# Two K chunks of a modulation product in one PE run, in a two-layer diffusion trunk on one NeuronCore

## The chip, the core and the metric

The kernel runs on one core of one Trainium2 chip. The metric is the device time of one execution in microseconds. Three runs of the kernel before took 1898.16, 1900.98 and 1904.77 us; the median is 1900.98.

## What is computed

The reference is a trunk of two layers over 256 latent tokens and 256 context tokens of width 1024. Each layer takes six modulation vectors from a conditioning vector, mixes the tokens in three branches (attention, a gated linear attention called GLA, a convolution), and ends in a feed-forward network. Cut to what matters here:

```python
mod = (silu_c @ w_ada[l] + b_ada[l])[:, None, :]
sh1, sc1, g1, sh2, sc2, g2 = jnp.split(mod, 6, axis=-1)
...
x = _post(x, _latent_mixer(_modulate(x, sh1, sc1), mem, cos, sin, p), g1, ln1_g[l], ln1_b[l])
x = _post(x, _ffn(_modulate(x, sh2, sc2), p), g2, ln2_g[l], ln2_b[l])
```

The product `silu_c @ w_ada[l]` has K = 1024 rows and 6144 columns. Its first 2048 columns (sh1, sc1) are made by one function, the other 4096 (g1, sh2, sc2, g2) by the one that is changed. The latent and the context conditioning vector are multiplied together, as the columns of one small stationary operand.

## The kernel before

PE does the large projections as three float32r products each: a weight chunk of 128 x 1024 values (512 KB) is loaded into a `raw` buffer by SP's queue (L107), ACT writes its rounded high part `whi` (L98), DVE the rest `wlo` (L99), and PE multiplies high by high, high by low and low by high (`mm`, L137). One feature-major group (`fm`, L153) is one such chunk and 24 matmuls. There are five `raw` buffers, three `whi` and two `wlo` (L54). A `raw` buffer of a weight chunk is free as soon as ACT and DVE have split it.

The modulation products are not split: they are plain float32 matmuls whose stationary operand is the conditioning vector (`self.sc[:, k, :]`, 128 x 32) and whose moving operand is the raw weight itself. Each output is 32 rows by 512 columns, and four of them (`gg` = 0 to 3) lie side by side on the 128 partitions of one PSUM bank. Their `raw` buffers come from the same five, and are free only when PE has multiplied them.

`ada_head` (L254) makes the first third of a layer's vectors, with its own operation line L280. In layer 0 it multiplies two K chunks for all four `gg` in one run of eight matmuls, from separate buffers and in the reverse order of loading. `ada_gen` (L294) makes the other two thirds, once with r = 1 and once with r = 2 for each layer, so it is called four times. It is a generator: at every `yield` it hands control back, and `step` (L872) takes one piece of it after each projection group, so that its transfers and products are spread between the groups. Behind the eighth piece it adds the bias (L311), transposes the sum through PE (L314), copies it into columns (L317) and stores two rows for later (L328).

The order of the work is the order of the program as a scheduler with priorities sorts it: weight loads and their splits are hoisted far ahead (`self.ahead = 3000`), evictions less far (`EVAC`), while the pieces of `ada_gen` stand about where they are written. Every engine and SP's queue then run in their fixed order.

The four calls lie in different surroundings. The first (layer 0, r = 1; 283 to 387 us in the trace) goes with the first half of the branch phase, where the convolution's taps (L679) and a GLA head share DVE. The second (layer 0, r = 2; from 484 us) goes with the convolution's branch, whose partial sums travel through DRAM (`mgold`, L1058, and `mgd`, L1066). The third and the fourth (layer 1, r = 1 and 2; 860 to 1000 us) are appended at L1162 behind `ada_head` of layer 1 and run in the feed-forward network of layer 0, with `raw<-in_wff` as the weight stream.

Of the kernel before, what the change touches and what calls it, by code (L numbers as in the profile page):

```python
# [21 lines left out]
KC = 8  # L22
# [30 lines left out]
class Trunk:  # L53
# [240 lines left out]
    def ada_gen(self, l, r, res):  # L294

        nc, I = self.nc, self.I
        ps = self.PS("mm")
        for k in range(KC):
            for hf in range(2):
                raw = self.T("raw", [128, 1152])  # L300
                c0 = (r - 1) * 2048 + hf * 1024
                nc.sync.dma_start(out=raw[:, :1024], in_=I["w_ada"][l, k * 128:(k + 1) * 128, c0:c0 + 1024])
                for g in range(2):
                    gg = 2 * hf + g
                    nc.tensor.matmul(ps[32 * gg:32 * gg + 32, :], self.sc[:, k, :], raw[:, g * 512:(g + 1) * 512],  # L305
                                     start=(k == 0), stop=(k == KC - 1))
            yield
        b = self.T("tB", [128, 512])
        nc.sync.dma_start(out=b, in_=I["b_ada"][l, r - 1])
        m = self.T("tB", [128, 512])  # L310
        nc.vector.tensor_tensor(out=m, in0=ps, in1=b, op=ALU.add)  # L311
        tr = self.PS("tr", (128, 4, 128))
        for t in range(4):
            nc.tensor.transpose(tr[:, t, :], m[:, t * 128:(t + 1) * 128], self.ident)  # L314
        mc = self.T("mc", [128, 32], name="modcol")
        for s in range(2):
            nc.vector.tensor_copy(  # L317
                mc[:, s * 16:(s + 1) * 16].rearrange("p (g t) -> p g t", g=4),
                tr.rearrange("p t (g s r) -> p s g t r", g=4, s=2)[:, s, :, :, 0])
        if r == 2:  # L320
            for s in range(2):
                nc.vector.tensor_scalar(out=mc[:, s * 16:s * 16 + 8], in0=mc[:, s * 16:s * 16 + 8],
                                        scalar1=1.0, scalar2=None, op0=ALU.add)

        for s in range(2):
            for n in range(2):
                row = 32 * (n + 2 * (r - 1)) + 16 * s
                nc.sync.dma_start(out=self.grow[2 * l + r - 1][s:s + 1, n * 512:(n + 1) * 512], in_=m[row:row + 1, :])  # L328
        res[(l, r)] = mc
        yield  # L330
# [961 lines left out]
```

## Time and profile before

| | |
|---|---|
| median of three runs | 1900.98 us |
| the profiled execution's own time | 1894.05 us |
| its span in the trace | 1892.3 us |
| granted TensorE clock, mean | 0.99 |
| TensorE (PE) busy | 1803.7 us, 95% |
| VectorE (DVE) busy | 1301.5 us, 69% |
| ScalarE (ACT) busy | 869.6 us, 46% |
| L305 on PE, 128 matmuls in 256 records | 35.1 us |
| bytes moved | 291.50 MB, 154 GB/s over the span |

The profile is one execution, traced. Busy time of PE counts pipelined matmuls with modelled ends, so a busy PE is not one at its peak. PEld is the load of stationary operands. A row of the groups by line names line, engine, operation, output and input tiles, shape and count, then busy time and mean duration in ns, then the idle time of the engine just before and what ended it. A row of the timeline starts with the start in us and the duration in us; a bracket at its end holds the idle time before it and its releaser. SPq is SP's DMA queue: its rows are issues, not transfers. An fp32 matmul leaves two records, so a run of four matmuls shows as x8.

### The profile page before, as it was taken

To read this page: it belongs to the slowest core of one execution; us is meant where nothing else is said; L and a number is where in the kernel's file an instruction comes from. 1 tells how busy PE (TensorE), PEld (TensorE's weight loads), DVE (VectorE), ACT (ScalarE), POOL (GpSimd) and SP (SyncE) were. 2 spreads that over 40 slices of the span, in tenths; PEclk is the share of its full clock that TensorE was granted. 3 is DMA by queue.
4 is the path that set the end of the run, shared out by engine and by line. 5 is a ranking of instruction groups with operands and counts; after the bars stand their busy time and mean duration, and the time that the engine had idled before them with its cause. 6 is when DMAs were issued, how large, how long until landed. Compare 5 with 4: busy or idle time off the path is not lost.

```text
span 1892.3 us, 29210 instructions
## 1 busy us (share of the span) xinstructions
PE 1803.7 (95%) x11260; PEld 1490.2 (79%) x11260; DVE 1301.5 (69%) x2266; ACT 869.6 (46%) x1498; POOL 189.9 (10%) x267
## 2 busy tenths in 40 slices
PE   6999999999999999989999999989999899979998
PEld 3777787777777878767768888877898789969996
DVE  4797999985743444864334457799999877676656
ACT  4455435434833333453222234556555476445442
POOL 0320000113002001000000001131000200210000
PEclk9999999999999999999999999999999999989999
DMA  8311124623374344576673367643233445755563
GB/s 322 99 56 56 57 69 142 206 85 91 122 253 134 101 135 145 196 259 219 204 240 107 103 214 237 210 126 91 91 112 116 143 128 164 238 196 172 195 205 120
DMA packets 90603, 291.50 MB, mean 154 GB/s; under 512 B 10320, under 2 KB 12112, under 8 KB 90464
## 3 DMA queue, kind: packets, MB, share of 16 engines
q1 hardware_dynamic: 90464, 289.64, 46.8%
q8 instruction: 88, 1.44, 0.3%
q14 instruction: 51, 0.42, 0.1%
HBM read 276.99 MB, written 12.62 MB: 153 GB/s over the span
## 4 chain that ended last, share of the span: by engine, by line
PE 74%; DVE 14%; ACT 5%; issue 3%; DMA 2%; POOL 2%; SPq 0%; POOLq 0%; DVEq 0%; ACTq 0%
PE mm L137 62%; DVE acc L679 5%; DVE wlo L99 4%; PE sd L453 2%; PE sd L427 2%; PE mm L305 1%; PE sd L614 1%; PE sd L641 1%; PE sd L561 1%; ACT whi L98 1%; PE sd L280 1%; PE tr L448 1%; DMA ada<-in_w_ada 1%; DMA raw<-in_wff 1%; DVE u L784 0%
## 5 line engine op out<-in xcount | busy, mean ns | idle before, releaser
L99 DVE TENSOR_TENSOR wlo<-raw,whi 128x1024 fp32r<-128x1024 f32 (+1 forms) x376 | 469.8, 1251 | 312.5 <-PE mm L137 221.8
L137 PE MATMUL mm<-hi,whi 128*128 128x512 f32 (+1 forms) x1904 | 649.8, 342 | 1.6 <-ACT whi L98 0.8
L137 PE MATMUL mm<-lo,whi 128*128 128x512 f32 (+1 forms) x1904 | 643.3, 338 | 3.1 <-DVE lo L358 2.9
L98 ACT ACTIVATE whi<-raw 128x1024 fp32r<-128x1024 f32 (+1 forms) x376 | 399.3, 1063 | 534.8 <-PE mm L137 384.2
L137 PE MATMUL mm<-hi,wlo 128*128 128x512 f32 (+1 forms) x1904 | 643.6, 338 | 0.5 <-DVE wlo L99 0.5
L137 PEld LDWEIGHTS mm<-hi,whi 128*128 128x128 f32 x1904 | 359.8, 189 | 59.7 <-issue 14.3
L137 PEld LDWEIGHTS mm<-lo,whi 128*128 128x128 f32 x1904 | 360.6, 189 | 45.6 <-DVE lo L358 6.9
L137 PEld LDWEIGHTS mm<-hi,wlo 128*128 128x128 f32 x1904 | 360.1, 189 | 39.2 <-issue 1.9
L679 DVE SCALAR_TENSOR_TENSOR acc<-y,cols,acc 128x512 f32<-128x512 f32 (+1 forms) x464 | 290.9, 627 | 9.6
L137 PE MATMUL mm<-wlo,hi 128*128 128x512 f32 (+2 forms) x676 | 239.6, 354 | 6.3 <-DVE wlo L99 6.3
L137 PE MATMUL mm<-whi,hi 128*128 128x512 f32 (+2 forms) x676 | 240.9, 357 | 1.3 <-ACT hi L356 1.3
L137 PE MATMUL mm<-whi,lo 128*128 128x512 f32 (+2 forms) x676 | 237.7, 353 | 0.0
L137 PEld LDWEIGHTS mm<-wlo,hi 128*128 128x128 f32 x676 | 127.8, 189 | 25.8 <-DVE wlo L99 8.4
L137 PEld LDWEIGHTS mm<-whi,hi 128*128 128x128 f32 x676 | 127.7, 189 | 20.7 <-ACT hi L356 2.3
L137 PEld LDWEIGHTS mm<-whi,lo 128*128 128x128 f32 x676 | 127.8, 189 | 17.3 <-DVE lo L358 1.2
L91 POOL TENSOR_SCALAR sm<-sm 128x1 f32<-128x1 f32 (+1 forms) x38 | 15.5, 408 | 727.7 <-DVE sm L336 648.2
L1064 POOL TENSOR_TENSOR mgp<-mgp,mgold 128x512 f32<-128x512 f32 x24 | 31.2, 1300 | 264.4 <-DVE mgp L1062 179.9
L687 POOL TENSOR_TENSOR csum<-csum,y 128x512 f32<-128x512 f32 (+1 forms) x14 | 16.8, 1201 | 395.4 <-DVE y L679 395.4
L453 PEld LDWEIGHTS sd<-pt,v 128*128 128x128 f32 x320 | 39.9, 191 | 15.7 <-ACT pt L450 11.6
L453 PE MATMUL sd<-pt,v 128*128 128x128 f32 x320 | 47.1, 286 | 2.8 <-ACT pt L450 1.5
L585 DVE TENSOR_TENSOR X<-X,sums 128x256 f32<-128x256 f32 (+1 forms) x112 | 45.7, 408 | 4.6 <-PE sd L561 2.8
L543 ACT ACTIVATE kk<-X 128x256 f32<-128x256 f32 x72 | 29.8, 419 | 37.8 <-DVE X L592 37.5
(234 smaller groups left out, 2053.2 us busy)
## 6 DMA issues: line engine op xcount, KB each, us to landing
raw<-in_wfm SPq DMA_DIRECT2D x112, 512.0 KB
raw<-in_wff SPq DMA_DIRECT2D x94, 512.0 KB
raw<-in_wdown SPq DMA_DIRECT2D x66, 512.0 KB
raw<-in_w_ada SPq DMA_DIRECT2D x64, 512.0 KB
raw<-in_wbr SPq DMA_DIRECT2D x48, 512.0 KB
ada<-in_w_ada SPq DMA_DIRECT2D x24, 512.0 KB
raw<-in_wout SPq DMA_DIRECT2D x24, 512.0 KB
raw<-in_wq SPq DMA_DIRECT2D x16, 512.0 KB
```

Source lines behind the costliest of these rows:

```text
L98: nc.scalar.activation(out=hi, in_=src, func=AF.Copy)
L99: (eng or nc.vector).tensor_tensor(out=lo, in0=src, in1=hi.bitcast(F32), op=ALU.subtract)
L137: i = self.nc.tensor.matmul(*a, **k)
L280: nc.tensor.matmul(ps[32 * g:32 * g + 32, :], self.sc[:, k, :], raw, start=(n0 == 0 and n < 4), stop=(l > 0 and n0 == 1 or n >= 4))
L305: nc.tensor.matmul(ps[32 * gg:32 * gg + 32, :], self.sc[:, k, :], raw[:, g * 512:(g + 1) * 512], start=(k == 0), stop=(k == KC - 1))
L427: nc.tensor.matmul(ps[:, :nk], qT[:, hh, :], self.kT[:, n, ko:512], start=True, stop=True)
L448: nc.tensor.transpose(tr[:, c, :], p[:, c * 128:(c + 1) * 128], self.ident)
L453: nc.tensor.matmul(po, self.v[:, ko // 128 + c, n * 128:(n + 1) * 128], pt[:, c, :], start=(c == 0), stop=(c == nkc - 1))
L543: nc.scalar.activation(out=cap(out[s], 0, [[2 * lev, nb], [lev, 2], [1, lev]]), in_=cap(X[s], W, [[2 * lev, nb], [2 * W + lev, 2], [1, lev ...
L585: nc.vector.tensor_tensor(out=a, in0=a, in1=t, op=ALU.mult)
L679: nc.vector.scalar_tensor_tensor(out=out, in0=win(y, sel, t), scalar=tap(t), in1=acc, op0=ALU.mult, op1=ALU.add)
L1064: nc.gpsimd.tensor_tensor(out=p, in0=p, in1=old, op=ALU.add)
```

## The change

`ada_gen` now goes over K in pairs of chunks. For each pair it issues the four transfers of 512 KB first (two chunks, two halves of the columns), collects the eight operands, and then multiplies them in reverse: the chunk and half loaded last comes first. The flag that starts an accumulation stands on the first four matmuls of the first pair, the flag that ends it on the last four of the last pair. There is one `yield` for a pair, so a call has four pieces where it had eight, each with four transfers and eight matmuls instead of two and four. The bias, the transposes and the stores are the same.

```diff
-        for k in range(KC):
-            for hf in range(2):
-                raw = self.T("raw", [128, 1152])
-                c0 = (r - 1) * 2048 + hf * 1024
-                nc.sync.dma_start(out=raw[:, :1024], in_=I["w_ada"][l, k * 128:(k + 1) * 128, c0:c0 + 1024])
-                for g in range(2):
-                    gg = 2 * hf + g
-                    nc.tensor.matmul(ps[32 * gg:32 * gg + 32, :], self.sc[:, k, :], raw[:, g * 512:(g + 1) * 512],
-                                     start=(k == 0), stop=(k == KC - 1))
+        for k0 in range(0, KC, 2):
+
+            parts = []
+            for k in (k0, k0 + 1):
+                for hf in range(2):
+                    raw = self.T("raw", [128, 1152])
+                    c0 = (r - 1) * 2048 + hf * 1024
+                    nc.sync.dma_start(out=raw[:, :1024], in_=I["w_ada"][l, k * 128:(k + 1) * 128, c0:c0 + 1024])
+                    parts += [(k, 2 * hf + g, raw[:, g * 512:(g + 1) * 512]) for g in range(2)]
+            for n, (k, gg, raw) in enumerate(parts[::-1]):
+                nc.tensor.matmul(ps[32 * gg:32 * gg + 32, :], self.sc[:, k, :], raw,
+                                 start=(k0 == 0 and n < 4), stop=(k0 == KC - 2 and n >= 4))
             yield
```

Three lines more shift the lines behind: the loads at L302 stand at L305 now, the matmuls at L308 instead of L305, the bias at L314, the transposes at L317.

On PE, in the third call, before, the end of one projection group, a run, and the start of the next group. `mm_8216` is the bank of the gate products, `raw_...` a buffer of w_ada, `sc` the conditioning vector; the other `mm` are banks of projection groups.

```order
L137 MATMUL mm_8316<-lo_7394,whi_8319 128x512
L137 MATMUL mm_8316<-hi_7393,wlo_8320 128x512
L305 MATMUL mm_8216<-raw_8347,sc 32x512 x2
L305 MATMUL mm_8216<-raw_8351,sc 32x512 x2
L137 MATMUL mm_8358<-hi_7379,whi_8361 128x512
L137 MATMUL mm_8358<-lo_7380,whi_8361 128x512
```

And of the change, at the last run of the same call, with the first instructions behind it. `tB` is the sum with the bias, `tr` the bank of its transposes.

```order
L137 MATMUL mm_8340<-hi_7393,wlo_8344 128x512
L308 MATMUL mm_8216<-raw_8377,sc 32x512 x2
L308 MATMUL mm_8216<-raw_8375,sc 32x512 x2
L308 MATMUL mm_8216<-raw_8373,sc 32x512 x2
L308 MATMUL mm_8216<-raw_8371,sc 32x512 x2
L137 MATMUL mm_8390<-hi_7379,whi_8393 128x512
L137 MATMUL mm_8390<-lo_7380,whi_8393 128x512
L317 MATMUL tr_8425<-ident,tB_8423 128x128 x4
```

A run has eight matmuls from four buffers, the one loaded last first. Between two runs stand 24 projection matmuls, before and now; behind the fourth run the next four groups have none. The transposes stand two matmuls behind the last run; before, the 24 matmuls of a whole group stood between.

On SP, in the third call, before. `in_wff` is the weight stream of the projection groups.

```order
L107 DMA raw_8273<-in_wff 128x1024
L302 DMA raw_8303<-in_w_ada 128x1024
L302 DMA raw_8307<-in_w_ada 128x1024
L107 DMA raw_8317<-in_wff 128x1024
L302 DMA raw_8347<-in_w_ada 128x1024
L302 DMA raw_8351<-in_w_ada 128x1024
L107 DMA raw_8359<-in_wff 128x1024
```

And of the change, at the same place:

```order
L107 DMA raw_8289<-in_wff 128x1024
L305 DMA raw_8319<-in_w_ada 128x1024
L305 DMA raw_8321<-in_w_ada 128x1024
L305 DMA raw_8323<-in_w_ada 128x1024
L305 DMA raw_8325<-in_w_ada 128x1024
L107 DMA raw_8341<-in_wff 128x1024
L305 DMA raw_8371<-in_w_ada 128x1024
```

Two transfers of w_ada to each weight chunk have become four. Before, the pair `raw_8303`, `raw_8307` waited for the buffers of the run two places ahead of its own; now the four from `raw_8319` on wait for the buffers of the run that stands one group ahead of theirs.

## Prediction

> **What bounds the kernel now.** I read the page's busy times and chain first, then the groups by line, the list of waits, the timeline around the gate products, and windows for the engines and the DMA.
>
> ```profile
> span 1892.3 us, 29210 instructions
> PE 1803.7 (95%) x11260; PEld 1490.2 (79%) x11260; DVE 1301.5 (69%) x2266; ACT 869.6 (46%) x1498; POOL 189.9 (10%) x267
> PE 74%; DVE 14%; ACT 5%; issue 3%; DMA 2%; POOL 2%; SPq 0%; POOLq 0%; DVEq 0%; ACTq 0%
> L98 ACT ACTIVATE whi<-raw 128x1024 fp32r<-128x1024 f32 (+1 forms) x376 | 399.3, 1063 | 534.8 <-PE mm L137 384.2
> L99 DVE TENSOR_TENSOR wlo<-raw,whi 128x1024 fp32r<-128x1024 f32 (+1 forms) x376 | 469.8, 1251 | 312.5 <-PE mm L137 221.8
> ```
>
> PE is busy for 95% and holds 74% of the chain: what is taken from PE's stream, or put into it as a wait, moves the end. The last two rows are the price of splitting one weight chunk, 1.06 us on ACT, then 1.25 us on DVE. Next the edited line, from the groups and the waits (total, times, longest).
>
> ```profile
> L305 PE MATMUL mm<-raw,sc 128*32 128x512 f32 x256 | 35.1, 604 | 0.0
> PEld mm L305 <- issue: 9.5, 27, 0.4
> ```
>
> Both records of a matmul are counted, so 256 are 128 products, in 32 runs of four. PE never sat idle for their data (0.0). They take 35.1 us of 1892: this is all that can be made shorter. The timeline between two runs of the third of the four calls, with SP's issues:
>
> ```profile
> 884.09 1.06 PE L305 MATMUL mm<-raw,sc 128*32 128x512 f32 x8
> 885.18 0.80 SPq L302 DMA_DIRECT2D raw<-in_w_ada  x2
> 887.24 0.33 SPq L107 DMA_DIRECT2D raw<-in_wff  x1
> 890.76 1.07 PE L305 MATMUL mm<-raw,sc 128*32 128x512 f32 x8
> ```
>
> A step lasts 6.67 us (890.76 - 884.09) and brings three transfers of 512 KB. The two gate transfers leave at 885.18, as the run at 884.09 ends, because it freed their buffers; by the order of SP they serve the run after next. They have nearly two steps, some 12.3 us, to land. That lead is what the change spends.
>
> ```profile
> 340.00:360.00 20.00, 19.63 (x102) 14.47 (x101) 19.14 (x47) 8.75 (x15) 0.00 (x0) 1.00 0.71 237
> 900.00:920.00 20.00, 20.00 (x98) 13.76 (x97) 7.12 (x8) 4.78 (x7) 0.00 (x0) 1.00 0.68 237
> ```
>
> Columns: length, busy PE, PEld, DVE, ACT, POOL, granted clock, DMA share, GB/s. In the first call (340) DVE is full beside PE; in the later ones (900) PE alone is.
>
> **The gain: 16 runs of eight for 32 of four.**
>
> ```profile
> 316.28 0.40 PE L137 MATMUL mm<-lo,whi 128*128 128x512 f32 x1
> 321.28 0.39 PE L137 MATMUL mm<-hi,wlo 128*128 128x512 f32 x1
> 24.23 1.92 PE L280 MATMUL sd<-ada,sc 128*32 128x512 f32 x16
> 25.31 0.80 SPq L272 DMA_DIRECT2D ada<-in_w_ada  x2
> ```
>
> Between 316.28 and 321.28 lie 22 projection matmuls: 5.00 / 22 = 0.227 us each, and the 24 of a group take 5.45. Of a step of 6.67, a run of four costs 6.67 - 5.45 = 1.22 us, though it lasts 1.07. A run of eight exists in the first layer's head (L280, 16 records): 1.92 us, 0.85 longer than one of four. So eight cost 1.22 + 0.85 = 2.07 against 2.44: 0.37 saved, and 16 times that is 5.9 us. The products themselves stay; the order within a run alone changes nothing, since no data was waited for.
>
> **The cost: lead.** There are five raw buffers. Four now belong to a run, and the next run's four transfers can leave only as this run frees them; the single group of 24 between two runs is their cover. That is 6.67 - 1.07 = 5.60 us. The row at 25.31 shows that half of a run of eight frees its buffers 1.08 us in: two transfers leave 0.84 us before the run's end, two at its end, and the weight chunk some 0.9 us after. How long do they need?
>
> ```profile
> 905.18 0.80 SPq L302 DMA_DIRECT2D raw<-in_w_ada  x2
> 907.78 0.33 SPq L107 DMA_DIRECT2D raw<-in_wff  x1
> 906.00:907.00 1.00, 1.00 (x6) 0.82 (x5) 0.74 (x2) 0.50 (x1) 0.00 (x0) 1.00 0.87 156
> 907.00:908.00 1.00, 1.00 (x6) 0.81 (x6) 0.76 (x1) 0.00 (x0) 0.00 (x0) 1.00 0.89 295
> 908.00:909.00 1.00, 1.00 (x6) 0.84 (x5) 0.00 (x0) 0.00 (x0) 0.00 (x0) 1.00 1.01 393
> 909.00:910.00 1.00, 1.00 (x7) 0.80 (x6) 0.00 (x0) 0.00 (x0) 0.00 (x0) 1.00 0.97 397
> 910.00:911.00 1.00, 1.00 (x8) 0.52 (x10) 0.00 (x0) 0.08 (x1) 0.00 (x0) 1.00 0.81 332
> ```
>
> Bytes begin 0.8 us after the first issue; then 156, 295, 393 and 397 KB in a us, 1241 KB in four, and about 0.395 MB/us from there. So bytes begin at the run's end. Four transfers (2.10 MB) are through 4 + 0.86 / 0.395 = 6.2 us after it, all five (2.62 MB) after 7.5.
>
> ```profile
> 860.48 2.51 SPq L302 DMA_DIRECT2D raw<-in_w_ada  x2
> 863.10 0.37 SPq L107 DMA_DIRECT2D raw<-in_wff  x1
> 863.57 3.75 SPq L302 DMA_DIRECT2D raw<-in_w_ada  x2
> 870.25 1.06 ACT L98 ACTIVATE whi<-raw 128x1024 fp32r<-128x1024 f32 x1 [7.03 <-DMA raw<-in_wff]
> 873.38 0.33 SPq L107 DMA_DIRECT2D raw<-in_wff  x1
> 876.95 1.06 ACT L98 ACTIVATE whi<-raw 128x1024 fp32r<-128x1024 f32 x1 [4.20 <-DMA raw<-in_wff]
> 876.00:877.00 1.00, 1.00 (x6) 0.84 (x5) 0.00 (x0) 0.05 (x1) 0.00 (x0) 1.00 0.13 49
> ```
>
> A lone chunk issued at 873.38 has its last bytes soon after 876.0 and is used at 876.95: 0.7 us from last byte to use. If transfers finish in the order of issue, the last gate transfer is usable 6.2 + 0.7 = 6.9 us after the run, and PE waits 1.3 us; if all five share the engines to the end, 8.2 and 2.6. The chunk issued third at 863.10 was usable only at 870.25, after 7.1 us, with two gate transfers issued after it: that leans to sharing. I take 1.9. The Trainium skill, "DMA: Bandwidth & Descriptors", section "Queues, rings and completion order", says that each engine consumes descriptors in ring order, which would keep the weight chunk behind the gates. By that alone the wait is the lower one, 1.3 us, and the sum below would be about 5 us smaller; the row at 870.25 does not settle it, but speaks against it.
>
> The weight chunk is usable at about 8.2 and needs 1.06 + 1.25 for its halves: 10.5. The next run ends at 5.6 + 1.9 + 1.9 = 9.4, and the third matmul behind it, half a us later, needs the low half: another 0.6 us, which delays the next run too and so eases its own wait, from 1.9 to 1.3. A full cycle loses 1.9 us in all. Behind a waiting run stands the next group on PE, and through it the evictions of ACT and DVE; behind the gate transfers on SP stands the next weight chunk, counted here. That the gate vector is complete after four steps instead of eight brings nothing, since its users come behind later phases.
>
> For a call of layer 0's FFN (the third and fourth): its first run is loaded long before; of the second run's four transfers one finds a buffer that a split had freed, so its wait is about 0.7; the third and fourth lose 1.9 each; the chunk behind the last run 0.6: 5.1 us. Four runs of eight give 1.5 back.
>
> ```profile
> 20.21 1.05 PE L288 MATMUL tr<-sel,m 128*128 128x2 f32 x8 [0.83 <-DVE m L285]
> 345.31 1.07 PE L305 MATMUL mm<-raw,sc 128*32 128x512 f32 x8
> 352.88 1.07 PE L305 MATMUL mm<-raw,sc 128*32 128x512 f32 x8
> 541.79 1.06 PE L305 MATMUL mm<-raw,sc 128*32 128x512 f32 x8
> 549.35 1.07 PE L305 MATMUL mm<-raw,sc 128*32 128x512 f32 x8
> ```
>
> In these two calls the four transposes of the result now stand two matmuls behind the last run; the row at 20.21 shows that a transpose just behind a copy of such a run waits 0.83 us. Less two matmuls of 0.227 that is 0.4. Each of the two calls: 5.1 + 0.4 - 1.5 = +4.0 us, together +8.0.
>
> The second call (541.79 to 549.35) has 7.56 - 1.07 = 6.5 us between runs, so its wait is 1.9 - 0.9 = 1.0, twice, the late chunk 0.6, and 256 KB transfers of the branch in the same queue, 0.65 us each by 0.395 MB/us, twice: 3.9 - 1.5 = +2.4. The first call (345.31 to 352.88) has the same 6.5, so 2.6 without the branch's traffic; but DVE, full in the window 340 to 360, works on while PE waits, and I let it give back 0.5: 2.1 - 1.5 = +0.6. Sum: 8.0 + 2.4 + 0.6 = **+11 us**. Bounds: with every full wait 1.3 and the late chunk hidden, (0.1 + 1.3 + 1.3 + 0.4 - 1.5) x 2 + (0.4 x 2 - 1.5) x 2 = about +2; with 2.6 + 0.6 for each full wait and 2.0 for the first, (2.0 + 3.2 + 3.2 + 0.6 + 0.4 - 1.5) x 2 + (2.3 x 2 + 0.6 - 1.5) x 2 + 1.3 = about +24.5. I stay below the middle, since a late chunk leaves more time to the gates behind it.
>
> The profiled execution took 1894.05 (span 1892.3) and would take 1905; the median of the runs is 1900.98, and the forecast is **1912 us**.
>
> **The rivals.** First, faster: the transfers land in time, and only the shorter runs are left, 1901.0 - 5.9 = 1895.1 us. It decides at 5.6 us of cover: four transfers within it need 2.10 MB in 5.6 us from the run's end, 0.375 MB/us with the landing inside; 397 KB/us was reached, but not from the start. For it: 0.0 us of idle in the row of L305. Against it: three transfers kept the DMA busy from 906 to 911 already. Chance 0.10.
>
> Second, no change: waits near the lower bound cancel the gain, +2 us, 1903. For it: the order of issue holds, and DVE or ACT catch up in the stalls. Against it: the row at 870.25. Chance 0.20.
>
> Third, worse: full sharing and a late chunk in each cycle, +24.5 us, 1925.5. It would be worse still if PE's clock fell in the waits:
>
> ```profile
> 800.00:820.00 20.00, 15.98 (x103) 11.01 (x101) 17.50 (x36) 11.65 (x21) 3.63 (x8) 0.91 0.82 268
> ```
>
> Here, with 4 us of idle, the granted clock averaged 0.91, which is 1.8 us lost in 20. The Trainium skill, "TensorE: Matmul & The Clock Gate", Part 1, puts the fall to half rate behind an idle window of about 3.4 us; waits of 1.3 to 2.6 us stay below it. Chance of this rival 0.20; the forecast has 0.50.
>
> **How the numbers follow.** A difference of 0.3% (5.7 us) is about what a measurement of this kernel can tell from none. Faster than that holds 0.08 (most of the first rival); within it 0.27 (0.02 of the first, the second, and 0.05 of the forecast's lower edge); slower 0.65. The range runs from near the first rival, 1897, to past the third with some 4 us of lost clock, 1930.
>
> **What would show it.** In the profile after, PE should wait for DMA of w_ada in front of the runs of eight, about ten times, 1 to 2 us each, most in the third and fourth call; runs of eight should last 1.9 us; a run's step should be near 9.4 us in the FFN. No such wait would make the first rival right; waits on the low halves of weights above 1 us each, or a clock below 1 in 860 to 1000, the third.

## The result, and the profile after

The changed kernel takes 1914.64 us, the median of four runs (1912.72 to 1921.44), against 1899.84 us for the kernel before in its runs so far (1898.16 to 1904.77). The ratio is 1.0094, with a 95% interval of 1.0074 to 1.0115: slower by 14.8 us by the two medians and by some 18 by the ratio. The forecast was 1912 us.

The traced execution of the changed kernel is its longest of four (1921.44 us), that of the kernel before lies below these four (1894.05 us). The two traces are 27 us apart where the medians are 15. So the reading below goes by stages, and compares a second trace of the changed kernel (1915.07 us) where that matters.

The page after, its span and busy times:

```profile
span 1919.7 us, 29192 instructions
PE 1814.1 (95%) x11260; PEld 1503.2 (78%) x11260; DVE 1299.8 (68%) x2266; ACT 867.0 (45%) x1496; POOL 190.4 (10%) x267
```

The instructions of PE are the same in number. The groups by line show the edited products, now on L308 (the new lines stand three further down), and the transposes of the result, four in each call:

```profile
L308 PE MATMUL mm<-raw,sc 128*32 128x512 f32 x256 | 32.8, 631 | 7.5 <-DMA raw<-in_w_ada 7.5
L317 PE MATMUL tr<-ident,tB 128*128 128x128 f32 x16 | 2.5, 276 | 0.3 <-DVE tB L314 0.3
```

Where the group of before ended in 0.0, PE now sits idle for 7.5 us for the loaded weights. That is only part of the loss. The list of waits (total, times, longest) for the changed kernel, then three rows of the kernel before that the prediction did not show:

```profile
PE mm L137 <- DVE wlo L99: 11.9, 16, 3.3
PE mm L308 <- DMA raw<-in_w_ada: 7.5, 5, 2.7
PE mm L137 <- ACT whi L98: 4.6, 8, 1.3
PE sd L486 <- DVE w L482: 4.1, 3, 2.7
```

```profile
PE mm L137 <- DVE wlo L99: 6.8, 7, 3.2
PE sd L483 <- DVE w L479: 1.6, 3, 0.7
PE mm L137 <- ACT whi L98: 0.8, 1, 0.8
```

The gate weights add 7.5 us, the low halves of the projection weights 11.9 - 6.8 = 5.1, their high halves 4.6 - 0.8 = 3.8, and `w` of L482, a small weight of the GLA branch, 4.1 - 1.6 = 2.5. Together 18.9 us of new waits, of which the shorter runs, and shorter waits elsewhere, give some back.

In the third call (under the feed-forward) the three steps between the four runs look like this on PE:

```profile
888.67 1.92 PE L308 MATMUL mm<-raw,sc 128*32 128x512 f32 x16
896.34 1.92 PE L308 MATMUL mm<-raw,sc 128*32 128x512 f32 x16
898.63 0.50 PE L137 MATMUL mm<-hi,whi 128*128 128x512 f32 x1 [0.37 <-ACT whi L98]
899.89 0.50 PE L137 MATMUL mm<-hi,wlo 128*128 128x512 f32 x1 [0.53 <-DVE wlo L99]
906.45 1.92 PE L308 MATMUL mm<-raw,sc 128*32 128x512 f32 x16 [1.28 <-DMA raw<-in_w_ada]
908.76 0.50 PE L137 MATMUL mm<-hi,whi 128*128 128x512 f32 x1 [0.39 <-ACT whi L98]
910.02 0.50 PE L137 MATMUL mm<-hi,wlo 128*128 128x512 f32 x1 [0.53 <-DVE wlo L99]
915.58 1.92 PE L308 MATMUL mm<-raw,sc 128*32 128x512 f32 x16 [0.27 <-DMA raw<-in_w_ada]
917.90 0.50 PE L137 MATMUL mm<-hi,whi 128*128 128x512 f32 x1 [0.40 <-ACT whi L98]
```

Steps of 7.67, 10.11 and 9.13 us. The first has no wait between its runs; the two others wait three times each: before the run for the gate weights, behind it for the high half of the next weight chunk, and 1.3 us later for the low half. What the queue did for the run at 906.45, from the timelines of SP, ACT and DVE and from windows of 1 us (the last three columns are the granted clock, the DMA share and GB/s):

```profile
897.43 1.75 SPq L305 DMA_DIRECT2D raw<-in_w_ada  x4
899.86 0.33 SPq L107 DMA_DIRECT2D raw<-in_wff  x1
```

```profile
898.61 1.22 DVE L99 TENSOR_TENSOR wlo<-raw,whi 128x1024 fp32r<-128x1024 f32 x1 [0.90 <-ACT whi L98]
907.65 1.06 ACT L98 ACTIVATE whi<-raw 128x1024 fp32r<-128x1024 f32 x1 [1.10 <-DMA raw<-in_wff]
```

```profile
898.00:899.00 1.00, 0.63 (x6) 0.30 (x2) 0.39 (x1) 0.58 (x1) 0.00 (x0) 1.00 0.69 82
899.00:900.00 1.00, 0.47 (x3) 0.11 (x2) 0.84 (x1) 0.00 (x0) 0.00 (x0) 1.00 0.90 287
...
901.00:902.00 1.00, 1.00 (x6) 0.84 (x5) 0.00 (x0) 0.00 (x0) 0.00 (x0) 1.00 1.01 410
...
904.00:905.00 1.00, 1.00 (x6) 0.63 (x4) 0.00 (x0) 0.00 (x0) 0.00 (x0) 1.00 1.00 401
905.00:906.00 1.00, 0.17 (x1) 0.00 (x0) 0.69 (x1) 0.07 (x1) 0.00 (x0) 1.00 0.75 299
906.00:907.00 1.00, 0.55 (x8) 0.25 (x12) 0.41 (x1) 0.56 (x1) 0.00 (x0) 1.00 0.06 25
```

The four transfers leave within the run at 896.34 and at its end. The weight chunk follows only at 899.86, as DVE has split the chunk before it (898.61 + 1.22) and so freed the fifth buffer. The engines then move up to 410 KB per us until the bytes end shortly after 906. The first three of the four land 3.8, 4.7 and 5.7 us after their issues, at 901.3, 902.5 and 904.0. The run, whose first product takes the fourth, can start at 906.45, and the weight chunk is usable at 907.65: both are late.

Time by stage needs borders. They are the first starts of instructions that the change does not touch; in the trace of before they lie at 285.0, 469.5, 619.8, 824.4 and 1265.1 us. The first call lies in the first stage, the second in the second, the third and fourth in 824 to 1265. Each number is the stage's length less that in the trace of before, in us:

| | 285-470 | 470-620 | 620-824 | 824-1265 | 1265-end |
|---|---|---|---|---|---|
| the changed kernel | +3.7 | +5.5 | +1.1 | +6.9 | +8.8 |
| the same, second trace | +4.9 | +5.1 | -0.1 | +7.6 | +0.6 |
| load order | +3.1 | +7.1 | +0.3 | +6.7 | +3.8 |
| two groups between runs | +0.3 | -1.2 | +0.7 | +1.1 | +4.8 |
| more buffers (feed-forward) | +3.2 | +3.3 | +0.4 | -4.8 | +5.6 |
| pairs in feed-forward calls only | +0.1 | 0.0 | +0.9 | +7.8 | +5.2 |
| pairs in layer 0's own calls only | +3.2 | +3.3 | +2.5 | +1.1 | +1.0 |
| before, no loads | -1.5 | -0.1 | +0.7 | -1.7 | +3.6 |
| after, no loads | -2.4 | -1.6 | +0.3 | -2.4 | +1.1 |
| feed-forward pairs, more buffers | +0.1 | -1.2 | +1.0 | -6.3 | +2.2 |
| that, and two groups in layer 0's own | -0.5 | +0.3 | +1.4 | -4.3 | +8.3 |
| runs of four, more buffers | 0.0 | -0.3 | +0.4 | -1.2 | +4.4 |
| w2 from a constant | +1.0 | +0.5 | +1.3 | +6.6 | +2.5 |

The last column holds nothing of the change: it runs from 0.6 to 8.8 in no order of the changes, is +4.4 for a kernel that has no run of eight there, and is never below the trace of before, whose execution took 5.8 us less than the median of its runs. Part of the largest is TensorE's clock: added up over windows of 2 us, the granted clock of that stage falls short of full speed by 13.0 us in the trace before, by 19.9 in that of the change and by 14.5 in its second trace. The loss of the change is in the other columns: 3.7 + 5.5 + 6.9 = 16.1 us. One trace of a stage is not exact either: in 824 to 1265 the traces with runs of four in the third and fourth call lie between -1.7 and +1.1.

### The profile page after: what moved, and what is told of

Its sections match the earlier page's. It is cut to its first block, busy times and chain, and to the rows that moved or that the text cites. A ratio compares the mean times of both kernels' runs of the same rounds, so it can differ in the third digit from the quotient of the medians.

```text
span 1919.7 us, 29192 instructions
## 1 busy us (share of the span) xinstructions
PE 1814.1 (95%) x11260; PEld 1503.2 (78%) x11260; DVE 1299.8 (68%) x2266; ACT 867.0 (45%) x1496; POOL 190.4 (10%) x267
```

## The experiments

The theory of the prediction: four of five buffers in one run leave the next run's transfers too little lead. The rivals were that the bandwidth itself is the bound, that the order of the products matters, and that the shift of later work against the shorter calls is what costs. Each run below is measured against the kernel before on the same chip.

### The changed kernel once more

No edit: a second trace and a second measurement.

> The changed kernel once more, for a second profile: in the first one, stages that the change does not touch were longer too (3.9 us between 423 and 470, 4.1 us between 1265 and 1528, 4.7 us in the tail). The theory (the lead of the gate transfers is too short) expects the time before plus 14 to 15 us, with the loss inside the four calls again (about 0, 5, and 7 to 8 us for the two in the feed-forward network) and the other stages as long as before. The rival (the new order shifts later stages) expects the same time, but the same 3.9, 4.1 and 4.7 us in the same stages.

Measured: 1913.45 us (6 runs) against 1897.54, ratio 1.0083, interval 1.0063 to 1.0102. The loss repeats, +16 us, and so do the stages of the calls in the second row of the table; the last column does not.

### Two groups between runs

```diff
+            yield
             yield
```

An empty step behind each pair puts two groups of 24 matmuls between two runs, as many projections per gate product as before.

> Runs of eight as in the change, but two projection groups between two runs instead of one, so that the next four transfers have 11 us instead of 5.6. Theory (lead): no wait for w_ada in front of a run, and the shorter runs alone remain: before minus 5.9 us, about 1894. Rival (the new order costs in later stages): before plus 5 or more. Rival (a wait of eight products on four transfers is dear in itself): slower than before.

Measured: 1898.47 us against 1897.54, ratio 1.0006, interval 0.9993 to 1.0019. The loss is gone. In the third call the runs are 13.00 us apart, with no wait:

```profile
882.45 1.92 PE L308 MATMUL mm<-raw,sc 128*32 128x512 f32 x16
895.45 1.92 PE L308 MATMUL mm<-raw,sc 128*32 128x512 f32 x16
908.45 1.92 PE L308 MATMUL mm<-raw,sc 128*32 128x512 f32 x16
```

Two steps of before are 13.34, so each pair saves 0.34. But the gain of 16 such pairs did not show in the total, which was a miss. Its waits say where part of it went:

```profile
PE mm L137 <- DVE wlo L99: 7.9, 9, 3.3
PE sd L487 <- DVE w L483: 4.3, 4, 2.7
```

4.3 us for the GLA branch's small weight against 1.6, and 7.9 for low halves against 6.8: 3.8 us of some 5 are given back, most of it in the stages of layer 0's own calls.

### The products in load order

```diff
-            for n, (k, gg, raw) in enumerate(parts[::-1]):
+            for n, (k, gg, raw) in enumerate(parts):
```

> The change without the reversal: the eight products in the order of loading. Theory (PE waits for the last landing of the four): a product can start as its own transfer lands, and behind the last landing only two products (0.5 us) are left instead of eight (1.92 us), so some 1.4 us less in each of about eight waiting runs: before plus 3 to 5 us. Rival (the run is interrupted by waits and loses what it gained): as the change, before plus 14 to 15 us.

Measured: 1916.36 us against 1897.54, ratio 1.0099, interval 1.0080 to 1.0118, which overlaps that of the repeat for most of its width. The expected +3 to +5 us was a miss, and the rival, as the change, came true: an effect of the order by itself is not shown. It only moves the waits: the gate products' fall to 2.3 us, a run in the third call stretches from 1.92 to 2.32 us, since it begins before its last data, and the matmul behind it then waits 1.26 us for the high half where the reversed order waited 0.37.

### More buffers under the feed-forward

```diff
-                    raw = self.T("raw", [128, 1152])
+                    raw = self.T("raw", [128, 1152]) if l == 0 or k == k0 else self.T("t4", [128, 1024])
```

> The change, but in the two calls in the feed-forward network the second chunk of each pair is loaded into buffers that lie idle there, so that a run's four transfers can leave two groups ahead; the bytes of a step stay the same. Theory (lead, from too few buffers): the waits of these two calls vanish and their cost goes from plus 7 or 8 us to minus 3, so before plus 3 to 5 us in all. Rival (bandwidth: 2.6 MB a step is more than the DMA moves in 7.5 us): the waits stay, before plus 12 to 15 us.

Measured: 1900.64 us against 1897.54, ratio 1.0020, interval 1.0008 to 1.0032. The same bytes in the same time, and under the feed-forward no wait for gate weights is left: that stage went from +6.9 to -4.8 (more than the 8 x 0.34 = 2.7 us that its eight runs can save; what the rest is stays open). So bandwidth is not the bound there; the buffers are. (The pool `t4` has four buffers, of which a run takes two.) What stays are the first two calls, +6.5 together.

### One half of the change at a time

```diff
-        for k0 in range(0, KC, 2):
+        if l == 1:
+            for k0 in range(0, KC, 2):
...
+        else:
+            for k in range(KC):
```

This one has pairs only in the two calls under the feed-forward; the next has `l == 0` in place of `l == 1`, so pairs only in the first and second call.

> Only the two calls under layer 0's feed-forward (the third and fourth) have the products of two chunks in one run; the first and second call are as before. Lead theory: two cycles each of about 1.3 to 2.6 us of waits, as the profile after shows them there (steps of 7.6 to 10.1 us where 7.5 has no wait), so that 824 to 1265 costs about 7 us more and nothing else does: +6.5 to +8 us. By the forecast's own term +8.0. Rival, that the time comes from the shift of everything behind the shorter calls (fewer steps in a call, so all later work stands elsewhere): nothing of the loss stays, since that shift is mostly in the first two calls: 0 to +2. The sum over this kernel and the one with pairs in layer 0's own calls should be that of the whole change, +15 to +16, if the two halves are independent.

> Only the first and second call have runs of eight; the calls under the feed-forward are as before. The forecast gave these two +0.6 and +2.4, together +3.0 us, with VectorE, full in the first call, giving back part of the wait. By the stages of the profiles after (285 to 470: +3.1 to +4.9; 470 to 620: +5.3 to +7.3 us) they cost +8 to +11 us. If the stages are right the run is +8 to +11, and the forecast had the two halves of the loss the wrong way round; if +3, the stages mislead and the loss is in the feed-forward alone.

Measured on one chip, against 1898.74 us: the feed-forward's half 1907.94, ratio 1.0044 (1.0029 to 1.0058); layer 0's own half 1908.36, ratio 1.0051 (1.0039 to 1.0063). That is +9.2 and +9.6 us, together 18.8 against 15 to 18 for the whole by its medians and ratios: the halves add up within their intervals. Work shifted by shorter first calls is not what the feed-forward loses by, since in the first of the two layer 0's own stages lose nothing (+0.1, 0.0) and the feed-forward keeps its +7.8. For the first two calls the kernel without loads, below, rules the shift out. And the first two calls are not the cheap half: the forecast's +3.0 for them falls. The second kernel's trace has 3.2 + 3.3 in their own stages and 2.5 more behind them, before 824.

### No loads

```diff
-                raw = self.T("raw", [128, 1152])
-                c0 = (r - 1) * 2048 + hf * 1024
-                nc.sync.dma_start(out=raw[:, :1024], in_=I["w_ada"][l, k * 128:(k + 1) * 128, c0:c0 + 1024])
+                raw = self.ident.unsqueeze(1).to_broadcast([128, 4, 128])
```

The same edit in the kernel before and in the changed one. Both leave out the loading of two thirds of `w_ada`.

> The kernel before, but the gate products of these calls take a constant tile that lies in the chip in place of the loaded weights: two thirds of w_ada (16.8 MB) is not read, the count and shape of the matmuls stay. It is the base for the next run. Lead theory: before, no gate product waited (0.0 us in the groups), so the loads cost TensorE nothing; but the weight chunks behind them in SP's queue come sooner, so -2 to -6 us by the few waits on weights and on the branch's transfers. Rival, bandwidth or SP's queue as a bound of the kernel before: -15 us or more.

> The changed kernel with the same constant in place of the loaded weights, so that runs of eight wait for no transfer. The gain alone should show: 16 times 0.37 us, 5.9 us less than the run before this one (runs of four, no loads), by the lead theory 4 to 6 us less. If instead it is equal or slower (0 or more), the runs of eight cost something that is no transfer: less work of TensorE between two runs leaves the splits of the weights on ScalarE and VectorE too little time, or the other branch's steps come earlier than their data; and then the loss of the change is only partly lead, some 6 us of it being order.

The expectation's 16.8 MB counts one layer only: 64 transfers of 512 KB are 33.6 MB. Measured: 1896.73 us for runs of four, ratio 0.9992 (0.9983 to 1.0001), and 1891.55 for runs of eight, ratio 0.9957 (0.9943 to 0.9971). Without transfers the change gains 1896.73 - 1891.55 = 5.2 us, as forecast (5.9). The order of the work is that of the change, with the same shorter calls, and the first two stages lose nothing (-2.4, -1.6): what the change loses needs the transfers. The steps on PE, runs of four first:

```profile
884.79 1.06 PE L303 MATMUL mm<-ident,sc 128*32 128x512 f32 x8
891.45 1.07 PE L303 MATMUL mm<-ident,sc 128*32 128x512 f32 x8
```

```profile
885.34 1.92 PE L306 MATMUL mm<-ident,sc 128*32 128x512 f32 x16
892.90 1.92 PE L306 MATMUL mm<-ident,sc 128*32 128x512 f32 x16
```

6.66 and 7.56: a run of eight costs 0.90 us more than one of four, so a pair saves 1.22 - 0.90 = 0.32, and 16 pairs 5.1.

### Two versions put together from these, and their control

Runs of eight only under the feed-forward, with half of their buffers from the pool `t4`; then the same with pairs and an empty step in layer 0's own calls; then the kernel before with only its buffers changed:

```diff
-                raw = self.T("raw", [128, 1152])
+                raw = self.T("raw", [128, 1152]) if l == 0 or k % 2 == 0 else self.T("t4", [128, 1024])
```

> Runs of eight only in the two calls under layer 0's feed-forward, and there the second chunk of each pair lies in two other idle buffers, so that the next run's transfers need not wait for this run; layer 0's own calls are as before. Lead theory: no wait stays and 8 runs save 0.37 us each, 3 us; in the kernel that had these buffers and pairs in all calls, 866 to 1265 took 2.4 us less than before and 824 to 1265 4.8 less. So -3 to -5 us against the kernel before. Rival, that these runs of eight bring nothing in a feed-forward where TensorE is full, and that the 4.8 were an execution's own: 0, within 2 us either way.

> Runs of eight in all four calls: under the feed-forward with the two other buffers, in layer 0's own calls with two groups of matmuls between two runs. Lead theory: both halves keep their gain, 8 x 0.37 each, but in layer 0's own calls the runs that had two groups between them measured -0.7 in the stages of that kernel's profile, so -4 to -6 us against the kernel before. Rival, that two groups between runs only move the wait to transfers that the other branch needs in the first two calls: no better than runs of eight under the feed-forward alone, -3.

> The kernel before, runs of four, but under the feed-forward every second chunk's loads go to the two other idle buffers. It tells whether a gain of the run of eight with more buffers is the run's or the buffers'. Lead theory: before, no gate product waited, so more buffers bring nothing by themselves, 0, at most -1 us from the 1.0 us of waits of the head of the next layer. If the buffers alone bring -3 to -5 us, the run of eight brings nothing, and the weight stream behind fewer held buffers is what gained.

Measured on one chip against 1898.65 us: the first 1895.60, ratio 0.9982 (0.9966 to 0.9998); the second 1898.94, ratio 1.0005 (0.9992 to 1.0018); the control 1898.57, ratio 1.0000 (0.9984 to 1.0016). The first is faster than both kernels, by 3 us, with an interval that just leaves out 1. Buffers alone bring nothing, which leaves the gain to the runs of eight, though the intervals of the first and of the control overlap. The steps of the first in the third call (a run of eight is two groups of records here, by their operand):

```profile
882.42 1.06 PE L309 MATMUL mm<-t,sc 128*32 128x512 f32 x8
883.30 1.04 PE L309 MATMUL mm<-raw,sc 128*32 128x512 f32 x8
889.98 1.06 PE L309 MATMUL mm<-t,sc 128*32 128x512 f32 x8
```

7.56 us apart, as with no loads at all. The second version was a miss: in the total, runs of eight in layer 0's own calls bring nothing even with two groups between them. In its trace their two stages stand at -0.5 and +0.3, and TensorE waits 3.6 us for `w` in place of 1.6.

### The GLA branch's small weight from a constant

```diff
-        nc.sync.dma_start(out=w[:, 0, :], in_=self.I["w2"][self.l, h])
-        nc.scalar.activation(out=w[:, 1, :].bitcast(F32R), in_=w[:, 0, :], func=AF.Copy)
+        nc.scalar.activation(out=w[:, 1, :].bitcast(F32R), in_=self.ident, func=AF.Copy)
...
-                                       in1=w[:, 0, :], op0=ALU.mult, op1=ALU.add)
+                                       in1=self.ident, op0=ALU.mult, op1=ALU.add)
```

The changed kernel, without the loads of `w2` (64 KB each). What led to it is the first call in the profile after, on SP, ACT and PE:

```profile
315.72 2.23 SPq L305 DMA_DIRECT2D raw<-in_w_ada  x3
318.04 0.38 SPq L479 DMA_DIRECT2D w2raw<-in_w  x1
318.51 0.40 SPq L305 DMA_DIRECT2D raw<-in_w_ada  x1
```

```profile
325.64 0.31 ACT L480 ACTIVATE w2raw<-w2raw 128x128 fp32r<-128x128 f32 x1 [4.86 <-DMA w2raw<-in_w]
```

```profile
326.48 0.61 PE L486 MATMUL sd<-glrT,w 64*128 64x512 f32 x2 [2.74 <-DVE w L482]
339.43 2.76 PE L308 MATMUL mm<-raw,sc 128*32 128x512 f32 x16 [2.35 <-DMA raw<-in_w_ada]
345.46 0.50 PE L137 MATMUL mm<-hi,wlo 128*128 128x512 f32 x1 [0.65 <-DVE wlo L99]
```

> The changed kernel, but the other branch's small weight w2 (64 KB, read four times in each layer in the same queue as the gate weights) is taken from a constant tile: its loading is left out. In the profile after, this load, issued between three gate transfers and the fourth, is used 7.6 us after its issue (5.9 before), and TensorE waits 2.7 us for its product in the first call (0.7 before). If the gate transfers delay the other branch in this way, the stage from 285 to 470, which grew by 3.1 to 4.9 us, grows by 2 us less, and the run is +11 to +13.5 us against the kernel before instead of +15 to +16. Rival, that the first call's loss is the wait for gate weights and late halves alone: the wait on w2 goes, but TensorE then waits as much longer for the next gate weights, and the run stays at +15 to +16.

Measured: 1907.08 us against 1896.84, ratio 1.0062, interval 1.0039 to 1.0084: +10.2 us where the whole change had +15 to +16. The interval overlaps that of the repeat, so the reading rests on the stages. Layer 0's two stages fell from +3.7 and +5.5 to +1.0 and +0.5, more than was expected, and the feed-forward kept its loss (+6.6). Part of the rival is seen as well: in the first call the gate products now wait 2.43 and 1.83 us in place of 2.35 once. The kernel before without these loads was not run; its own waits for `w` were 1.6 us in all, so some of the fall is not the change's.

## Why the prediction was right, and where its parts were wrong

Slower by lost lead came true, and the time lies inside the range; the size, +11 us, was 4 to 5 us short of the +15 to +16 measured. That 1912 lies within 3 us of 1914.64 is in part luck: it stands on a median of 1900.98 us, and later medians of the kernel before were 1896.84 to 1898.74. Point by point:

**The gain** of 5.9 us holds: 5.2 us measured without loads, with a run of eight at 1.92 us and a pair saving 0.32 to 0.34 instead of 0.37.

**The lead** is shown. With two groups of cover, or with half of each run's buffers from another pool, the gate waits under the feed-forward go; with no loads at all, the change gains.

**The feed-forward calls**, forecast at +8.0, measured +6.9 and +7.6 by stages, and +9.2 us as a half alone. The waits of the third call are 0.1 in its first step, 10.11 - 7.56 = 2.55 and 9.13 - 7.56 = 1.57 in the others, and some 0.8 behind the last run: 5.0 us, where the forecast had 5.1 for a call. The fourth call has 4.5 by the same count, and 9.5 less 8 x 0.32 is 6.9, the measured stage. The 0.4 us for the transposes in each of these two calls did not come: L317 waits 0.3 us in all four calls together, 1.4 in the second trace, and never under the feed-forward.

**How a full cycle's loss is made up** was sized wrong, though its sum was right (1.9 forecast; 2.55 and 1.57 in the third call, 1.29 and 2.35 in the fourth). The gate wait is 1.3 us or less there. That is not because the gates were early: the last of them was usable 8.2 us after the run's end (898.26 to 906.45) and 7.2 in the next step (908.37 to 915.58), where the forecast had 6.9 to 8.2. But the halves of the weight chunk behind the run come late by 0.4 us at the high half, which the forecast took as hidden, and by 0.5 at the low half (0.6 forecast), and with these waits the cover is 6.9 us instead of 5.6. The chunk also left 1.6 us after the run's end (899.86) and not 0.9, since its buffer waits for the split of the chunk before.

The rows answer the question between the two bounds as well: the four gate transfers and the chunk behind them end one after the other, at 901.3, 902.5 and 904.0, by 906.45 and by 907.65, so the engines do not share to the end. "DMA: Bandwidth & Descriptors" of the Trainium skill, section "Queues, rings and completion order", says that each engine takes descriptors in ring order; these rows agree with it. The order does not make the sum 5 us smaller, as the prediction worked out from it, since the time that the gates do not wait the chunk behind them does.

**The first two calls** were the step that failed: +0.6 and +2.4 forecast, +3.7 and +5.5 measured. Behind the gate transfers on SP stands not only the next weight chunk but also the branch's small weight, which the prediction counted as bytes at most and not as something that PE waits for. That wait and the clock were missing from its sum. In the first call the new waits are 2.74 - 0.69 = 2.05 us for `w`, 2.35 for the gates, 0.65 for a low half and 0.3 for the transposes. The other engines did give time back, more than the 0.5 forecast for DVE: PE's other waits in the stage fell from 7.1 to 5.1 us. Together PE's idle time grew by 3.35 us (184.5 - 176.7 = 7.8 before, 188.2 - 177.05 = 11.15 after). The shorter runs take off 1.3, and the clock, below, adds about 1.7: 3.75, and the stage measured 3.7. In the second call the gates cost 2.67 once, high and low halves 2.9 more, and `w` 0.5, less 1.3: 4.8 of 5.5. That the transfers of `w2` are the way in which the loss comes is shown by the constant in their place only in sum; how much of it is the change's alone stays open.

**The clock** of the changed kernel under the feed-forward, and then in the first call, from windows (the third number from the end):

```profile
836.00:1284.00 448.00, 436.46 (x2211) 351.30 (x2207) 235.10 (x320) 169.70 (x235) 25.02 (x38) 1.00 0.56 187
320.00:340.00 20.00, 14.91 (x100) 9.08 (x102) 16.91 (x42) 10.06 (x16) 1.49 (x1) 0.91 0.69 240
328.00:329.00 1.00, 1.00 (x8) 0.20 (x4) 1.00 (x3) 1.00 (x3) 0.00 (x0) 0.50 0.00 0
340.00:360.00 20.00, 19.02 (x131) 12.82 (x122) 16.82 (x29) 8.35 (x12) 0.00 (x0) 0.91 0.72 266
```

Before, the first call's windows had 1.00:

```profile
320.00:340.00 20.00, 19.31 (x152) 12.45 (x151) 19.43 (x37) 12.33 (x17) 1.49 (x1) 1.00 0.65 217
```

Under the feed-forward the mean stayed at 1.00. In the first call it did not: just behind the wait of 2.74 us that ends at 326.48, and again 1 us behind that of 2.35 that ends at 339.43, the granted clock fell to 0.50 for some 3.4 us each time, and the runs of eight that fell into these spells lasted longer than 1.92 us:

```profile
327.73 3.09 PE L308 MATMUL mm<-raw,sc 128*32 128x512 f32 x16
```

The other took 2.76. So the prediction's statement that waits of 1.3 to 2.6 us are too short for this does not hold here. Added up over windows of 2 us the clock of the stage from 285 to 470 falls short by 3.4 us (5.1 in the second trace) where before it was 1.7, from a spell at 381 to 385 behind a wait of 2.62. The wait of 2.67 us in the second call was not followed so at once; there the clock fell 5 us later, behind shorter waits, for as long as it did in that stage before. The fall in the first call is the forecast's worse rival in a small part, and in a place where the prediction did not look. With `w2` from a constant the shortfall is 1.7 us as well, so some of that experiment's gain in the first stage is clock.

The signs named beforehand came in part: runs of 1.92 us, and full feed-forward steps of 10.11, 9.13, 8.85 and 9.91 (mean 9.5, 9.4 forecast), but five waits for the gates instead of ten, and the rest at the weights behind them.

## What to carry to other kernels

Joining two short runs on PE saves the switch between them, here 0.3 us, but it also ties twice the buffers to one moment: count how many buffers are free of the run, and what the next run's transfers have left as cover, before counting the saving. Buffers of another pool brought the gain back where PE alone was the bound, and a longer gap did so in the steps but not in the total. When a burst of large transfers is put together, look behind it in the queue, at the next weight and at the smallest transfer of another branch, for there more than half of the new waits stood. And look at the clock where a wait on PE grows past 2 us: here two such waits were followed by half speed.

## What was not expected of the hardware

A transfer of 64 KB issued in the middle of four of 512 KB was used 7.6 us after its issue (318.04 to 325.64), just behind the third of the large ones, which landed at 325.35: its size did not bring it forward. The last two of the five large ones of a cycle under the feed-forward were usable 1.2 us apart, while the engines moved about 400 KB per us. PE's granted clock halved behind waits of 2.74 and 2.35 us. Reading 33.6 MB less, in the kernel before, changed its time by 2.0 us of 1898.74, with an interval that holds no change.
